# A meter for the projection work, and the written order on TensorE, in a hybrid HGRN2 + RWKV-7 layer

## The chip, the cores and the metric

The kernel runs on one core of a Trainium2 chip. A core has a matrix engine (TensorE, "PE" in the profile, with its weight loads as "PEld"), a vector engine (VectorE, "DVE"), an activation engine (ScalarE, "ACT"), GpSimd ("POOL") and a sync engine ("SP"). The last two are used here almost only to issue DMA transfers; a "q" behind an engine's name means its queue of transfers. The metric is the time of one execution in device microseconds, as the median of several runs; lower is better.

## What is computed

One decoder layer over 2048 tokens of width 1024, in float32. The input projection feeds two recurrent mixers side by side, HGRN2 (four heads of 128) and RWKV-7 (eight heads of 64). Their outputs go through an output projection; then comes a gated feed-forward network with a causal convolution of width 3.

```python
h = rmsnorm(x);  proj = h @ w_in            # 1024 -> 3840 columns
o_hg = hgrn2(q, f, i, g)                    # S_t = diag(f_t) S_{t-1} + k_t v_t^T ; o_t = S_t^T q_t
o_rw = rwkv7(r, k, v, wd, ad, gd)           # S_t = S_{t-1} diag(w_t) + (S_{t-1} a_t) b_t^T + v_t k_t^T
x = x + concat(o_hg, o_rw) @ w_out
x = x + conv_ffn(rmsnorm(x))                # 1024 -> 2 x 2816, conv over 3 tokens, SiLU gate, -> 1024
out = rmsnorm(x)
```

## The kernel before, in words

Tokens are worked on in four blocks of 512. To keep float32 precision with the fast matmul form, each operand of a projection is split into a high part (a copy on ScalarE) and a low part (a subtraction on VectorE); one product is then three matmuls of 128x512 (`mm3`, lines 259 to 261: high x high, high x low, low x high). Splits of weights are lines 243 and 244, other splits 236 and 237.

**Stage 1** (`phase1`) holds the input projections, both recurrences and the output projections of the first three blocks. Three generators are run against each other. Each `yield` ends a step.

- `dense()` goes through a list of jobs: 30 column blocks of the input projection for each token block ("P", eight steps of one `mm3` each, into the PSUM tag `pj`); transposes of the next block's input ("T", `turn`, line 428); the output projection of a finished block ("O", `out_block`, 32 steps of one `mm3` each); norms and transposes for stage 2 ("N"). Weights come by POOL's queue through tiles `wraw`/`woraw` and split tiles `wh` and `wl`, four buffers of each. `load(i)` fetches the two pairs of split tiles for column block `i`, one block ahead: read and split in the first token block, read back already split from DRAM in the later ones.
- `rw_super()` does RWKV-7 for one token block and four of the eight heads: eight such super steps, numbered 0 to 7 here, each a chain over all engines. Its main stations are: decay and keys (L647 to L694); scores `M` (matmuls L706, mask on VectorE L709); transposes (L731, L740, L745) and L757; the inverse of the triangular score matrices (below); L802, L815, L828 that put the inverse together and apply it; L852 with the VectorE evictions L855 and L858; L868 and L875 into two more PSUM banks; eight chunk steps (L886, with L888 on VectorE); then L896, L904, L916 and the output `yo` (L917, L918, stored by L919).
- `hg_unit()` does HGRN2 for one token block and one head: sixteen units, with VectorE products (L945 to L954), score matmuls (L970), transposes (L1012) and a state update (L1025).

**The inverse** is solved on VectorE with another layout than the scores have. Parts of `M` are stored to DRAM (`Ed`, L722) and read back as `E` (L725). A loop of 31 dependent pairs of VectorE instructions (L776, L778) makes `Ti`, with a `yield` after every fourth. `Ti` is stored (`T0d`, L782), and so is a transposed copy `TiT` (`T1d`, L785). Both are read back in the scores' layout, as `TZ` (L790, read by L802) and `TTs` (L794, read by L815 and L828). All these transfers are issued by SP in the order of the text.

**What sets the order.** The main loop takes one step of the RWKV-7 stream and one of the HGRN2 stream, then `fill(TICK)` takes steps of `dense()` worth 2000 ns of their own price (648 for an `mm3`, 680 in an output block, 436 for four transposes). A scheduler then orders each engine's instructions by its own estimate of when they are ready, TensorE's too, so that the order on an engine can differ from the text. An output block waits until both recurrences have finished its token block.

**Stage 2** begins with the output projection of the last block (`wacc`, its loads at L1153 from `oT`), then up-projection, convolution and down-projection, with a Strassen-like scheme. Its buffers lie where those of stage 1 lay.

Of the kernel before, what the change touches and what calls it, by code (L numbers as in the profile page):

```python
# [25 lines left out]
NFF = FF // P  # L26
TICK = 2000.0
NEG_C = -0.6065306597126334
# [30 lines left out]


@with_exitstack
def tile_layer(ctx, tc, consts, x, norm1_w, w_in, hg_lb_logits, hg_norm_w, rw_shift_mu, rw_w0, rw_w2,
# [3 lines left out]
    nc = tc.nc  # L66
    V, S, TE = nc.vector, nc.scalar, nc.tensor
    dma = nc.sync.dma_start
# [40 lines left out]
    def act(out_, in_, func, **kw):  # L109

        want = tables.get(func)
        if want is not None and want != tab["now"]:
            pre = S.preload_act_table_set(want)
            for u_ in tab["uses"]:
                tc.add_manual_dep(pre.ins, u_.ins.name, NOSYNC, reason="table order")
            tab.update(now=want, pre=pre, uses=[])
        i_ = S.activation(out_, in_, func, **kw)  # L117
        if want is not None:
            tc.add_manual_dep(i_.ins, tab["pre"].ins.name, NOSYNC, reason="table order")
            tab["uses"].append(i_)  # L120
        return i_
# [141 lines left out]
    def phase1(c1):  # L263
# [102 lines left out]

        def out_block(nb, oh=None, ol=None, then=None):


            for i2 in range(2):  # L370
                for dh in range(2):
                    accs = [bank("pj") for _ in range(2)]
                    for k in range(KD):
# [16 lines left out]
                        for q in range(2):  # L390
# [4 lines left out]
                            if i2 == 1 and dh == 1 and q == 1:  # L395
                                next_block(then, k)
                            yield 680
                    for q in range(2):
# [100 lines left out]
        def dense():  # L499
# [64 lines left out]
            for n, jb in enumerate(jobs):  # L564
# [14 lines left out]
                if jb[0] in "OW":  # L579
                    while done["rw2"] < 2 * jb[1] + 2 or done["hg"] < 4 * jb[1] + 4:  # L580
                        yield None
                    if jb[0] == "W":
                        jb[2]()
                    else:
                        yield from (out_block(2, *rows["O"]) if jb[1] == 2 else out_block(jb[1], then=jb[1] + 2))
                    continue
# [5 lines left out]
                if i == 0:  # L592
                    next(ahead)
                    next(ahead)
                    constants()
                load(i + 1)
                i += 1
# [32 lines left out]
        def rw_super(nb, s_):  # L630
# [84 lines left out]
            Ed = dp.tile([64, 32, 32], F32, tag="Ed", name="Ed", bufs=2)  # L715
            T0d = dp.tile([2, 64, 32, 16], F32, tag="T0d", name="T0d", bufs=2)
            T1d = dp.tile([64, 16, 2, 32], F32, tag="T1d", name="T1d", bufs=2)
# [6 lines left out]
            for f in range(2):  # L724
                dma(E[64 * f:64 * f + 64], Ed)  # L725

            KBT = tile_("KBT", [2, 8, P], "KBT")
# [53 lines left out]
            TiT = rp.tile([P, 16, 32], F32, tag="E", name="TiT")  # L781
            dma(T0d.rearrange("f m t c -> (f m) t c"), Ti)  # L782
            act(TiT, Ti.rearrange("m a b -> m b a"), AF.Copy)
# [3 lines left out]
            for e in range(2):  # L787
                r0 = er0(e)
                for f in range(2):
                    dma(TZ[r0:r0 + 32, 0].rearrange("p u b h t -> p (u b h) t")[:, :, 16 * f:16 * f + 16],  # L790
                        T0d[f, 32 * e:32 * e + 16].rearrange("m t c -> t m c"))
                for q in range(2):
                    m0 = (e * 2 + q) * 16
                    dma(TTs[r0 + 32 * q:r0 + 32 * q + 32, :, 32 * q:32 * q + 32],  # L794
                        T1d[m0:m0 + 16].rearrange("m c f t -> (c f) m t"))
            for _ in range(2):
                yield
            z = bank2()
# [278 lines left out]

        while any(alive.values()):
            for key, g in (("r", rw_), ("h", hg_)):
                if alive[key]:  # L1080
                    try:
                        next(g)
                    except StopIteration:
                        alive[key] = False
            fill(TICK)


    if "1" in stages:
        with ExitStack() as c1:
            phase1(c1)  # L1090
# [420 lines left out]
```

## Time and profile before

| | |
|---|---|
| median of 3 runs | 2753.06 us (2752.97 to 2757.32) |
| the profiled execution | 2757.5 us, of which the span from first to last instruction is 2755.7 us |
| TensorE busy | 96% of the span |
| VectorE busy | 69% |
| ScalarE busy | 49% |
| mean granted TensorE clock | 0.983 |

A page of the profile names engines as above and source lines as L12. "Idle before" is time in which an engine did nothing before an instruction, put down to what ended it. Ends of matmuls are modelled, and matmuls overlap in the pipeline, so the start of the next one tells more of a matmul's cost than its own duration. The chain of waits is followed back from the last instruction, at each step to whatever released it. Views by stretch give each engine's busy microseconds, then the clock that TensorE was granted (1.00 is full), then the share of DMA time and GB/s.

### The profile page before, as it was taken

The page shows a single profiled execution, that of the slowest core. Times are in us where ns is not written, and L with a number is a line of the kernel's source. Part 1 is how long each engine was busy: PE and PEld are TensorE (multiplying, and loading weights), DVE is VectorE, ACT ScalarE, POOL GpSimd, SP SyncE. Part 2 cuts the span into 40 slices and gives each one's busy share as a digit, 9 for nine tenths or more (in the row PEclk, how much of TensorE's full clock was granted, in tenths as well). Part 3 has the DMA queues.
Part 4 walks back from the last instruction along what each step waited for, and adds up shares of the span by engine and source line. Part 5 has one row for each costly group of instructions (what it writes and reads, how often), then busy time and mean ns, then how long its engine had stood idle before and what let it go on. Part 6 is the DMA issues. An engine that isn't in the chain of part 4 may idle for free.

```text
span 2755.7 us, 47958 instructions
## 1 busy us (share of the span) xinstructions
PE 2647.8 (96%) x18059; PEld 2107.5 (76%) x18059; DVE 1898.6 (69%) x3665; ACT 1350.4 (49%) x2164; POOL 368.3 (13%) x660
## 2 busy tenths in 40 slices
PE   7999999989999999999989999998999999999998
PEld 6777777767777767778667788886888888877887
DVE  4856556565456664657657889988997786667656
ACT  5546443444544444344446755455455555445444
POOL 6433222212321113222100000000000000000000
PEclk9999999999999999999999999999999999999999
DMA  8645544355663546844575367746662224999865
GB/s 301 202 152 166 165 138 131 115 146 173 217 176 104 152 146 203 286 138 123 161 273 160 114 205 258 242 148 218 223 228 77 88 85 144 327 327 313 285 196 184
DMA packets 364285, 515.78 MB, mean 187 GB/s; under 512 B 97311, under 2 KB 193941, under 8 KB 364053
## 3 DMA queue, kind: packets, MB, share of 16 engines
q1 hardware_dynamic: 312113, 343.29, 38.6%
q0 software_dynamic: 51872, 169.41, 18.9%
q8 instruction: 142, 2.33, 0.3%
q14 instruction: 90, 0.74, 0.1%
q10 hardware_dynamic: 68, 0.02, 0.0%
HBM read 375.22 MB, written 137.36 MB: 186 GB/s over the span
## 4 chain that ended last, share of the span: by engine, by line
PE 73%; DMA 8%; DVE 7%; issue 5%; ACT 4%; SPq 1%; POOL 1%; DVEq 0%; ACTq 0%; POOLq 0%
PE pj L259 8%; PE pj L260 7%; PE pj L261 7%; PE ua L261 5%; PE ua L259 5%; PE ua L260 5%; PE ud L259 3%; PE ud L260 3%; PE ud L261 3%; PE da L260 2%; PE da L261 2%; PE da L259 2%; PE hg L970 2%; PE db L259 2%; PE db L261 2%
## 5 line engine op out<-in xcount | busy, mean ns | idle before, releaser
L259 PE MATMUL pj<-hh,wh 128*128 128x512 f32 x960 | 404.9, 422 | 0.7 <-ACT hh L117 0.7
L261 PE MATMUL pj<-hh,wl 128*128 128x512 f32 x960 | 380.6, 397 | 0.0
L260 PE MATMUL pj<-hl,wh 128*128 128x512 f32 x960 | 380.6, 397 | 0.0
L259 PE MATMUL ua<-Bh,uwh 128*128 128x512 f32 x704 | 278.6, 396 | 13.8 <-ACT uwh L243 13.1
L261 PE MATMUL ua<-Bh,uwl 128*128 128x512 f32 x704 | 276.9, 394 | 0.9 <-DVE uwl L244 0.9
L260 PE MATMUL ua<-Bl,uwh 128*128 128x512 f32 x704 | 276.4, 393 | 0.0
L259 PEld LDWEIGHTS pj<-hh,wh 128*128 128x128 f32 x960 | 182.4, 190 | 54.2 <-issue 11.8
L260 PEld LDWEIGHTS pj<-hl,wh 128*128 128x128 f32 x960 | 182.6, 190 | 39.7 <-issue 6.2
L261 PEld LDWEIGHTS pj<-hh,wl 128*128 128x128 f32 x960 | 182.2, 190 | 40.1 <-issue 0.4
L243 ACT CAST uwh<-uraw 128x512 fp32r<-128x512 f32 x220 | 134.8, 618 | 145.9 <-PE ua L260 73.2
L243 ACT CAST dah<-draw 128x512 fp32r<-128x512 f32 x151 | 93.8, 621 | 184.1 <-PE da L260 50.5
L244 DVE TENSOR_TENSOR uwl<-uraw,uwh 128x512 fp32r<-128x512 f32 x220 | 146.7, 684 | 47.5 <-ACT uwh L243 47.3
L244 DVE TENSOR_TENSOR dal<-draw,dah 128x512 fp32r<-128x512 f32 x151 | 104.0, 689 | 107.3 <-ACT dah L243 107.2
L259 PEld LDWEIGHTS ua<-Bh,uwh 128*128 128x128 f32 x704 | 133.6, 190 | 43.1 <-ACT uwh L243 13.7
L261 PEld LDWEIGHTS ua<-Bh,uwl 128*128 128x128 f32 x704 | 133.5, 190 | 30.6 <-DVE uwl L244 2.7
L260 PEld LDWEIGHTS ua<-Bl,uwh 128*128 128x128 f32 x704 | 133.6, 190 | 27.3
L259 PE MATMUL ud<-Bh,uwh 128*128 128x512 f32 x352 | 137.9, 392 | 1.9 <-DVE cv L1362 1.9
L261 PE MATMUL ud<-Bh,uwl 128*128 128x512 f32 x352 | 137.1, 389 | 0.0
L260 PE MATMUL ud<-Bl,uwh 128*128 128x512 f32 x352 | 137.0, 389 | 0.0
L260 PE MATMUL da<-dbl,dah 128*128 128x512 f32 x340 | 133.8, 394 | 0.6 <-DVE dbl L244 0.5
L261 PE MATMUL da<-dbh,dal 128*128 128x512 f32 x340 | 133.3, 392 | 0.0
L259 PE MATMUL da<-dbh,dah 128*128 128x512 f32 x340 | 128.3, 391 | 2.4 <-ACT dbh L243 2.3
(558 smaller groups left out, 6036.7 us busy)
## 6 DMA issues: line engine op xcount, KB each, us to landing
uraw<-in_w_up_dram SPq DMA_DIRECT2D x176, 256.0 KB, 3.3
woraw<-in_w_out_dram POOLq DMA_DIRECT2D x96, 256.0 KB, 3.6
draw<-Sg SPq DMA_DIRECT2D x88, 256.0 KB, 3.1
draw<-Tw SPq DMA_DIRECT2D x88, 256.0 KB, 3.0
gd<-y SPq DMA_DIRECT2D x86, 256.0 KB, 2.9
xt<-x1d SPq DMA_DIRECT2D x32, 512.0 KB, 6.0
draw<-gd SPq DMA_DIRECT2D x63, 256.0 KB, 4.8
draw<-in_w_down_dram SPq DMA_DIRECT2D x63, 256.0 KB, 5.3
```

The costliest lines, as they stand in the source:

```text
L243: S.copy(hi, src)
L244: V.tensor_sub(lo, src, hi.bitcast(F32))
L259: TE.matmul(acc, lh, rh, start=first, stop=False, skip_group_check=skip)
L260: TE.matmul(acc, lh, rl, start=False, stop=False, skip_group_check=skip)
L261: TE.matmul(acc, ll, rh, start=False, stop=last, skip_group_check=skip)
L970: TE.matmul(o, kt[:, t0:t0 + 64], qs, start=True, stop=True, tile_position=(0, e * 64))
```

## The change

Four things are changed; the arithmetic is the same.

1. The order of TensorE's instructions in stage 1 is the order in which the text issues them. The other engines are ordered by the scheduler as before.
2. The projection work of a tick is no longer a constant 2000 ns. A wrapper around VectorE adds up an estimate for each instruction issued (150 ns plus 1.04 ns an element of a row), half that for each ScalarE activation, and 8000 ns at two places where `rw_super` sends data through DRAM. A tick then grants 900 ns plus 0.45 of what the two recurrence steps of this tick have added. One of two empty steps ahead of L802 is gone.
3. `T0d` has the two halves of a row next to each other. The store of `Ti` becomes two transfers with pieces of 64 bytes, the four loads of `TZ` become two with pieces of 128 bytes, and all of them are issued ahead of the four loads of `TTs`.
4. The weights of the column block that follows an output block are no longer loaded ahead of that block, but in its last quarter, three steps of eight before the end.

```diff
-TICK = 2000.0
+FLOOR, RATE = 900.0, 0.45
+OP_NS, ELEM_NS, TRIP_NS = 150.0, 1.04, 8000.0
...
+def width(ap):
+    n = 1
+    for d in ap.shape[1:]:
+        n *= d
+    return n
+
+class Metered:
+    def __init__(self, engine):
+        self.engine, self.ns = engine, 0.0
+
+    def __getattr__(self, name):
+        call = getattr(self.engine, name)
+
+        def f(out_, *args, **kw):
+            self.ns += OP_NS + ELEM_NS * width(out_)
+            return call(out_, *args, **kw)
+
+        return f
...
-    V, S, TE = nc.vector, nc.scalar, nc.tensor
+    S, TE = nc.scalar, nc.tensor
+    V = Metered(nc.vector)
...
+        V.ns += 0.5 * (OP_NS + ELEM_NS * width(out_))
         i_ = S.activation(out_, in_, func, **kw)
...
-        def out_block(nb, oh=None, ol=None, then=None):
+        def out_block(nb, oh=None, ol=None, then=None, last=None):
...
                             if i2 == 1 and dh == 1 and q == 1:
                                 next_block(then, k)
+                                if k == KD - 3 and last is not None:
+                                    last()
...
-                        yield from (out_block(2, *rows["O"]) if jb[1] == 2 else out_block(jb[1], then=jb[1] + 2))
+                        yield from (out_block(2, *rows["O"]) if jb[1] == 2 else
+                                    out_block(jb[1], then=jb[1] + 2, last=lambda: load(i)))
...
-                load(i + 1)
+                kinds = [jb_[0] for jb_ in jobs[n + 1:]]
+                if "O" not in kinds[:kinds.index("P") if "P" in kinds else 0]:
+                    load(i + 1)
...
-            T0d = dp.tile([2, 64, 32, 16], F32, tag="T0d", name="T0d", bufs=2)
+            T0d = dp.tile([64, 32, 2, 16], F32, tag="T0d", name="T0d", bufs=2)
...
             for f in range(2):
                 dma(E[64 * f:64 * f + 64], Ed)
+            V.ns += TRIP_NS
...
-            dma(T0d.rearrange("f m t c -> (f m) t c"), Ti)
+            for f in range(2):
+                dma(T0d[:, :, f, :], Ti[64 * f:64 * f + 64])
             act(TiT, Ti.rearrange("m a b -> m b a"), AF.Copy)
...
-                for f in range(2):
-                    dma(TZ[r0:r0 + 32, 0].rearrange("p u b h t -> p (u b h) t")[:, :, 16 * f:16 * f + 16],
-                        T0d[f, 32 * e:32 * e + 16].rearrange("m t c -> t m c"))
+                dma(TZ[r0:r0 + 32, 0].rearrange("p u b h t -> p (u b h) t"),
+                    T0d[32 * e:32 * e + 16].rearrange("m t f c -> t m (f c)"))
+            for e in range(2):
+                r0 = er0(e)
                 for q in range(2):
                     m0 = (e * 2 + q) * 16
                     dma(TTs[r0 + 32 * q:r0 + 32 * q + 32, :, 32 * q:32 * q + 32],
                         T1d[m0:m0 + 16].rearrange("m c f t -> (c f) m t"))
-            for _ in range(2):
-                yield
+            V.ns += TRIP_NS
+            yield
...
         while any(alive.values()):
+            t0 = V.ns
...
-            fill(TICK)
+            fill(FLOOR + RATE * (V.ns - t0))
...
-        with ExitStack() as c1:
+        with ExitStack() as c1, tc.manual_schedule(engines={mybir.EngineType.PE}):
             phase1(c1)
```

## The prediction

> **What bounds the kernel now.** I read the page first, then the waits of TensorE, then the stretches with a low granted clock, then the instructions in order of time at three places.
>
> ```profile
> span 2755.7 us, 47958 instructions
> PE 2647.8 (96%) x18059; PEld 2107.5 (76%) x18059; DVE 1898.6 (69%) x3665; ACT 1350.4 (49%) x2164; POOL 368.3 (13%) x660
> ```
>
> TensorE is the bound, so a change that leaves its 18059 matmuls alone can only win what TensorE loses: idle time, half clock, and matmuls that run long. Stage 2's instructions are the same in both programs, so all of it must come from stage 1 and its end, about the first 1400 us. The idle time, by what ended it:
>
> ```profile
> PE pj L259 <- ACT wh L243: 14.7, 12, 4.3
> PE rw L802 <- DMA TZ<-T0d: 14.3, 9, 4.3
> PE rw L868 <- DVE AR L858: 8.9, 6, 2.2
> PE wacc L259 <- ACT Bh L236: 7.3, 1, 7.3
> PE hg L1012 <- DVE hk L1005: 3.9, 1, 3.9
> PE rw L815 <- ACT TZ L117: 2.0, 4, 0.5
> ```
>
> Columns: us in total, times, longest. Five places hold most of it: split output weights (L259), the solved inverse coming back from DRAM (L802, L815: 16.3 us), PSUM banks after L858, and the border to stage 2. The clock comes on top:
>
> ```profile
> 157.00:171.00 14.00, 14.00 (x182) 9.86 (x180) 6.43 (x18) 10.52 (x26) 2.33 (x4) 0.52 0.30 114
> 597.00:611.00 14.00, 9.72 (x179) 6.91 (x179) 5.48 (x15) 4.56 (x12) 0.95 (x2) 0.53 0.60 126
> 1384.00:1405.00 21.00, 13.74 (x47) 10.39 (x46) 12.07 (x18) 8.90 (x14) 1.27 (x2) 0.76 0.66 231
> ```
>
> Columns: stretch, length, busy us of PE, PEld, DVE, ACT, POOL, then granted clock. Around the L802 steps of two super steps the clock is half; 14 x (1 - 0.52) = 6.7 us is the most such a stretch costs.
>
> **Part 1: the written order on TensorE.** The scheduler of before moves projections in between the small matmuls. In the built programs the number of runs of 512-column projections that begin behind other work falls from 298 to 240 in stage 1. What a new run costs:
>
> ```profile
> 1371.49 0.72 PE rw L896 x18
> 1372.21 0.43 PE pj L259
> 1372.64 0.23 PE pj L260
> 1372.87 0.24 PE pj L261
> ...
> L259 PE MATMUL pj<-hh,wh 128*128 128x512 f32 x960 | 404.9, 422 | 0.7 <-ACT hh L117 0.7
> L260 PE MATMUL pj<-hl,wh 128*128 128x512 f32 x960 | 380.6, 397 | 0.0
> ```
>
> The chain of waits shows the first projection behind a small matmul at 0.43 us, its followers at 0.23: 0.20 us a run, 58 x 0.20 = 12 us saved. The lower bound is the group rows: L259, which begins each run, is busy 24.3 us more than L260, 0.08 a run over 298 runs, 5 us. I take 12, the single case seen directly. [...]
>
> L868 follows L852 with no projection between in six of eight super steps of before, and waits 8.9 us for the banks that L858 empties. The written order puts three projection steps or more there, of three matmuls each (9 x 0.23 = 2.1 us, against 1.5 us a wait). Gain 9; lower bound 4, if VectorE is behind.
>
> In exchange TensorE may no longer pass a matmul that isn't ready. Recurrence and HGRN2 matmuls of the same tick now hold up whatever is written behind them. Before shows this at one place only (L1012, 3.9 us once); between nothing and 4 us in each of the eight super steps, I take 5 in total, near the one row, and keep 0 to 32.
>
> **Part 2: the meter, and the inverse's round trip.** Each tick now grants 900 ns plus 0.45 of the VectorE time that the step is estimated to have issued, instead of 2000 ns. What counts is whether the work written between the score matmuls (L706) and L802 covers the chain behind L802: copy to DRAM and back, 31 dependent pairs on VectorE (L776, L778), and copy again. Super step 3:
>
> ```profile
> 546.46 1.29 DVE L709 TENSOR_TENSOR M<-rw,cst 128x512 f32<-128x512 f32 x2 [2.75 <-PE rw L706]
> 559.27 0.19 DVE L776 TENSOR_TENSOR etmp<-E,Ti 128x31 f32<-128x31 f32 x1
> 593.30 0.16 DVE L778 TENSOR_TENSOR Ti<-Ti,etmp 128x16 f32<-128x16 f32 x1
> ...
> 600.35 0.31 PE L802 MATMUL rw<-TZ,M 32*32 32x32 f32 x4 [0.34 <-DMA TZ<-T0d]
> 603.32 1.06 PE L802 MATMUL rw<-TZ,M 32*32 32x32 f32 x60 [2.65 <-DMA TZ<-T0d]
> ```
>
> ```profile
> 559.27:593.46 34.19, 33.33 (x255) 26.41 (x256) 30.84 (x110) 15.45 (x28) 7.09 (x13) 1.00 0.47 147
> ```
>
> So 11.5 us from the last mask product to the loop, 34.2 us of loop (VectorE busy for 30.84 of it, the third number behind the stretch's length), and 10 us from its end to the last L802 operand: 55.6 us in all, and 3.0 us of wait. The loop is long because other VectorE work stands in it:
>
> ```profile
> L244 DVE TENSOR_TENSOR wl<-woraw,wh 128x512 fp32r<-128x512 f32 x94 | 64.5, 688 | 46.9 <-ACT wh L243 46.2 <-ACT hv L117 0.2
> L778 DVE TENSOR_TENSOR Ti<-Ti,etmp 128x126 f32<-128x126 f32 (+22 forms) x248 | 62.4, 252 | 3.5
> L776 DVE TENSOR_TENSOR etmp<-E,Ti 128x126 f32<-128x126 f32 (+22 forms) x248 | 61.8, 249 | 15.5 <-DMA E<-Ed 12.2
> L945 DVE TENSOR_TENSOR hX<-hq,hf 128x256 f32<-128x256 f32 x112 | 46.9, 419 | 3.3 <-PE hg L970 2.8
> ```
>
> From the built programs: between L706 and L802 stand 1244 projection matmuls before and 1320 after over the eight super steps (+76 x 0.23 = +17 us of cover), but 123 fewer HGRN2 matmuls (about 0.09 us each, -11) and 29 fewer runs (-6). Cover in total is unchanged. Inside the loops the foreign VectorE instructions go from 335 to 311, but unevenly. In super step 1 they fall from 50 to 29. In steps 3 and 5 the projection side's rise from 12 to 23 and from 11 to 24, because the output block now falls into the loop: 11 to 13 more at 0.69 us less some HGRN2 work at 0.42 is 6 us more loop in each. Step by step, the old wait plus the loop's change minus the cover's change gives (0 to 7) 3, 0, 5, 8, 0, 4, 6, 0: 26 us against 14 before at L802. I book +12; the ends are -16 (all gone) and +35 (each step waits as step 3 does).
>
> **Part 3: the changed layout of the round trip.** One store of the inverse (256 KB) becomes two with 64-byte pieces; four loads become two with 128-byte pieces, and both now stand on SP ahead of the four L794 loads, which wait for a second store.
>
> ```profile
> T0d<-Ti SPq DMA_DIRECT2D x8, 256.0 KB, 2.1
> TZ<-T0d SPq DMA_DIRECT2D x32, 32.0 KB, 2.8
> DMA to landing us min/median/max: 2.9/3.6/4.0
> ```
>
> The last row is of the neighbour T1d, whose stores have 128-byte pieces. The new store resembles those more than the old one: I take 4 to 5 us to land, 2 to 3 more than 2.1. In return the second half of TZ is no longer queued behind L794 (2.65 us in the row of 603.32). Booked at 0, ends -3 and +3 us in each super step that waits. The L794 loads come later by two issues; L815 needs them after L802's matmuls, its operands' evictions and a projection step, which cover that.
>
> **Part 4: weights around the output blocks.** Before loads the next projection's weights ahead of each output block, and they hold two of four buffers through it; that is where most of L259's 14.7 us fall. After, four are free, and the load is issued three k-steps before the end. The third block has all four already and waits some 2 us; so I take 14.7 to 8, gain 7. Ends: 12 gained, or 5 lost if the late load (four transfers on POOL's queue) isn't there when the next projection starts. Late next is the split itself.
>
> **Part 5: the border.**
>
> ```profile
> 1390.16 0.39 PE L261 MATMUL pj<-wh,hl 128*128 128x512 f32 x1
> 1397.80 0.79 PE L259 MATMUL wacc<-woh,Bh 128*128 128x512 f32 x1 [7.25 <-ACT Bh L236]
> ...
> 1387.90 1.22 DVE L918 TENSOR_TENSOR yo<-rw,yo 128x1024 f32<-128x1024 f32 x1
> 1396.91 0.69 DVE L237 TENSOR_TENSOR wol<-Bl,woh 128x512 fp32r<-128x512 f32 x1 [5.64 <-ACT woh L236]
> ...
> 1394.03 3.02 DMA Bh<-oT
> ```
>
> In before the last work is the third output block, and stage 2's loads wait for its last matmul (3.02 us of landing in the open). After, that block is done first and the loads wait only for the matmul 36 places before the end, so they lie under the last recurrence steps. What remains open is L918 and two splits, 2.6 us, plus two ScalarE passes in the last super step that projections covered: 5 us against 7.25. With half of the 21 x 0.24 = 5 us of lost clock: gain 4.5 (0 to 10).
>
> **The sum**, against the profiled execution's 2757.5 us: -12 - 9 + 5 + 12 - 7 - 4.5 = -15.5, so 2742. The median shown lies 4.4 us below that execution, so 2737.
>
> **The rivals.** *The round trip is covered everywhere.* If the meter spreads the cover well and the loops with fewer foreign instructions (step 1) are typical, L802's 16 us go as well and nothing new waits: -12 - 9 - 12 - 4.5 - 16 = -54, 2700. Against it: steps 3 and 5.
>
> *VectorE becomes the bound of the recurrence (slower).* TensorE in order stands at an HGRN2 or output matmul whose operand is queued on VectorE in the loop; projections behind it, and so their evictions, come late, and with them the rest of the loop. It decides once the waits at and before L802 pass 16 + 33 + 6 = 55 us, 7 us a super step instead of 2. At 9 a step it is 72 - 16 - 33 = +23: 2776. For it: VectorE is busy for 30.84 of the 34.19 us loop shown; against it: the foreign instructions fall in sum.
>
> *The clock takes it back (no change).* Four waits of 4 us and more at L802 (steps 2, 3, 5, 6) could each bring a stretch as at 157 us: 4 x 6.7 less the two that before has already is +13, so 2751. [...]
>
> **How the numbers follow.** This kernel can tell about 0.2% (5.5 us) from no change. Forecast 0.42 (2737, own range 2722 to 2747), all covered 0.18, VectorE 0.28, clock 0.12. Faster 0.60, same 0.12, slower 0.28. The range of 2703 to 2775 leaves out the better part of "all covered" and the worse half of "VectorE".
>
> **What would show it.** Right: L868 and L259 nearly gone from the waits, fewer and longer runs of pj, wacc's first wait under 5 us, L802 at about 25 us with steps 3 and 5 longest. Wrong: waits of pj or hg on VectorE above 20 us in sum, L802 above 50, or new slices of low clock.

## The result, and the profile after

The changed kernel takes 2806.16 us (median of 4 runs, 2804.15 to 2808.43) against 2755.19 us for the kernel before on the same chip (median of 4, 2752.97 to 2760.16). The ratio is 1.0181, with a 95% interval of 1.0167 to 1.0196: slower, where 2737 was forecast. Its profiled execution has a span of 2805.7 us, 50.0 us more than before.

From the page of the changed kernel (busy time of each engine, share of the span, instructions):

```profile
PE 2643.6 (94%) x18059; PEld 2109.4 (75%) x18059; DVE 1910.3 (68%) x3665; ACT 1366.7 (49%) x2178; POOL 367.1 (13%) x660
```

TensorE is busy for 4.2 us less than before, and the span is 50.0 us longer: by this row all of the loss is waiting. (Busy time at half the clock counts as busy, though: in a row of the last section PE is busy for 3.40 of 3.40 us at a granted clock of 0.50.) Where the loss lies is seen from stage 1 alone, from 20 us to the first wacc matmul. One row of the windows view for each kernel gives the length, then the busy us of PE, PEld, DVE, ACT and POOL, then the granted clock. Before:

```profile
20.00:1397.80 1377.80, 1315.11 (x12240) 1017.54 (x12241) 834.35 (x2046) 624.89 (x1000) 353.65 (x633) 0.98 0.53 168
```

The changed kernel, the whole stage and then a stretch of 13.7 us in the first super step:

```profile
20.00:1445.00 1425.00, 1314.93 (x12252) 1023.26 (x12250) 844.57 (x2043) 643.08 (x1016) 352.57 (x632) 0.95 0.53 163
148.30:162.00 13.70, 3.26 (x73) 2.65 (x72) 2.27 (x7) 2.57 (x6) 3.00 (x5) 0.63 0.84 206
```

Stage 1 ends 47.2 us later; 2.8 us of the 50.0 are lost behind it. Its length splits into three parts, which I use for every kernel below: *idle* (length less busy TensorE: 62.7 before, 110.1 after), *half clock* (half of TensorE's busy time in the stretches that the records show at half the clock: 26.2 and 48.7) and the *remainder* (1288.9 and 1266.2). So by this split the changed kernel loses 47 us more to waits and 22 us more to the clock, and 23 us less are left for the matmuls at full clock: 47.4 + 22.5 - 22.7 = +47.2. Half is an upper bound, and every us too much in it is missing in the remainder; for the projections it is nearly reached, since in such a stretch one starts 0.43 us behind the other (median), and 0.23 us outside. The half clock comes in 20 stretches with 130 us in sum, against 11 with 63 us.

The waits of TensorE in the changed kernel (us in total, times, longest; L836 is before's L802, L285 to L287 are L259 to L261, L456 is L428, L886 is L852; all VectorE work carries the meter's L80):

```profile
PE rw L836 <- DMA TZ<-T0d: 40.7, 12, 10.1
PE pj L285 <- ACT wh L269: 16.2, 8, 5.3
...
PE pj L456 <- ACT xt L143: 8.2, 5, 3.8
PE pj L285 <- DVE hgg L80: 7.4, 3, 3.3
PE pj L286 <- DVE wl L80: 7.0, 15, 2.4
PE rw L886 <- ACT UV L143: 5.7, 2, 3.1
PE hg L279 <- DVE xt L80: 5.2, 3, 3.0
PE pj L285 <- DVE xh L80: 4.0, 2, 2.1
PE wacc L285 <- ACT Bh L262: 3.0, 1, 3.0
PE hg L1046 <- DVE hk L80: 2.9, 1, 2.9
PE pj L285 <- DVE Sc L80: 2.6, 1, 2.6
```

Set against the rows of before: the round trip at L802 rises from 14.3 to 40.7. The wait at L868 (8.9) is gone, since its successor L902 has no row any more. The split weights of projections and output blocks rise from 16.5 (14.7 on wh, 1.8 on wl) to 23.2. New are projection matmuls that wait until VectorE has emptied a PSUM bank (hgg, xh and Sc, 14.0 in sum; the Sc copy stands right behind an addition of xh, which empties the bank), the transposes of the next input, which wait for ScalarE's copies (L456: 8.2, before's L428 2.2), and matmuls of the recurrence whose operand is late (L886).

Two of these waits in order of time. First the longest one at L836. The chain in the queue of SP (start, length, issued work), where the inverse is done at 143.1 us:

```profile
143.15 4.63 SPq L815 DMA_DIRECT2D T0d<-Ti  x2
147.82 7.05 SPq L818 DMA_DIRECT2D T1d<-TiT  x2
156.75 0.84 SPq L822 DMA_DIRECT2D TZ<-T0d  x2
158.13 1.95 SPq L828 DMA_DIRECT2D TTs<-T1d  x4
```

and TensorE beside it:

```profile
148.32 0.39 PE L287 MATMUL pj<-hh,wl 128*128 128x512 f32 x1
158.76 0.32 PE L836 MATMUL rw<-TZ,M 32*32 32x32 f32 x4 [10.06 <-DMA TZ<-T0d]
```

The projections written between the score matmuls and L836 are used up at 148.7 us; the next instruction in the written order is L836, and TensorE stands for 10.06 us. The issue of the two stores takes 4.63 and 7.05 us of SP's time, and the loads stand behind them.

Second, the longest wait on split weights, in super step 7, where an output block lies in front of L836:

```profile
1371.97 0.54 POOL L409 DMA_DIRECT2D woraw<-in_w_out_dram  x1 [3.71 <-DVE wl L80]
1375.24 0.62 ACT L269 CAST wh<-woraw 128x512 fp32r<-128x512 f32 x1 [2.75 <-DMA woraw<-in_w_out_dram]
1375.89 0.69 DVE L80 TENSOR_TENSOR wl<-woraw,wh 128x512 fp32r<-128x512 f32 x1 [0.55 <-ACT wh L269]
...
1376.80 1.90 SPq L828 DMA_DIRECT2D TTs<-T1d  x4
1376.88 0.54 POOL L409 DMA_DIRECT2D woraw<-in_w_out_dram  x1 [4.37 <-DVE wl L80]
...
1378.74 0.96 SPq L429 DMA_DIRECT2D x1d<-xh  x2
1379.80 5.58 SPq L406 DMA_DIRECT2D oraw<-oT  x4
1383.03 0.40 ACT L262 CAST hh<-oraw 128x256 fp32r<-128x256 f32 x1 [7.17 <-DMA oraw<-oT]
1383.31 0.54 POOL L409 DMA_DIRECT2D woraw<-in_w_out_dram  x1 [5.89 <-DMA x1d<-xh]
1383.34 0.61 ACT L269 CAST wh<-woraw 128x512 fp32r<-128x512 f32 x1
```

One turn of a weight buffer runs POOL's issue, landing, ScalarE's copy, VectorE's subtraction, and then the next issue, which waits for that subtraction: from 1371.97 to 1376.88 it is 4.91 us. The four buffers of the ring serve the loads of the other half (oraw) and the output rows (xh) too. At 1376.80 SP is busy with the round trip's loads, xh is stored at 1378.74 and oraw is asked for at 1379.80, behind them. ScalarE waits 7.17 us for oraw, and the copy of the weights follows behind that split, at 1383.34. TensorE's matching row is "5.3" in the waits above. So the work that the meter gives as cover for the round trip is fed in part through the same SP queue as the round trip. No run moves these transfers to another queue, so what the sharing costs is not shown.

### The profile page after: what moved, and what is told of

The parts are those of the page before. It is cut to its first block, busy times and chain, and to the rows that moved or that the text cites. A ratio compares the mean times of both kernels' runs of the same rounds, so it can differ in the third digit from the quotient of the medians.

```text
span 2805.7 us, 47910 instructions
## 1 busy us (share of the span) xinstructions
PE 2643.6 (94%) x18059; PEld 2109.4 (75%) x18059; DVE 1910.3 (68%) x3665; ACT 1366.7 (49%) x2178; POOL 367.1 (13%) x660
## 4 chain that ended last, share of the span: by engine, by line
PE 41%; DMA 3%; DVE 3%; issue 1%; ACT 1%; SPq 1%; DVEq 0%; ACTq 0%
PE ua L285 5%; PE ua L287 5%; PE ua L286 5%; PE ud L285 3%; PE ud L286 3%; PE ud L287 3%; PE da L286 2%; PE da L287 2%; PE da L285 2%; PE db L285 2%; PE db L286 2%; PE db L287 2%; PE ub L285 1%; PE ub L287 1%; PE ub L286 1%
## 5 line engine op out<-in xcount | busy, mean ns | idle before, releaser
L285 PE MATMUL pj<-hh,wh 128*128 128x512 f32 x960 | 411.0, 428 | 0.1
L287 PE MATMUL pj<-hh,wl 128*128 128x512 f32 x960 | 380.2, 396 | 0.0
L285 PE MATMUL ua<-Bh,uwh 128*128 128x512 f32 x704 | 278.5, 396 | 16.2 <-ACT uwh L269 14.1
L287 PE MATMUL ua<-Bh,uwl 128*128 128x512 f32 x704 | 276.5, 393 | 0.5 <-DVE uwl L80 0.4
L285 PEld LDWEIGHTS pj<-hh,wh 128*128 128x128 f32 x960 | 183.6, 191 | 51.5 <-issue 8.8
L287 PEld LDWEIGHTS pj<-hh,wl 128*128 128x128 f32 x960 | 183.2, 191 | 40.9
L80 DVE TENSOR_TENSOR uwl<-uraw,uwh 128x512 fp32r<-128x512 f32 x220 | 146.7, 684 | 50.2 <-ACT uwh L269 50.1
L80 DVE TENSOR_TENSOR dal<-draw,dah 128x512 fp32r<-128x512 f32 x151 | 104.0, 689 | 103.9 <-ACT dah L269 103.5
L285 PEld LDWEIGHTS ua<-Bh,uwh 128*128 128x128 f32 x704 | 133.2, 189 | 45.7 <-ACT uwh L269 14.7
L287 PEld LDWEIGHTS ua<-Bh,uwl 128*128 128x128 f32 x704 | 133.2, 189 | 30.8 <-DVE uwl L80 2.8
L285 PE MATMUL ud<-Bh,uwh 128*128 128x512 f32 x352 | 137.9, 392 | 1.4 <-DVE cv L80 1.4
L287 PE MATMUL ud<-Bh,uwl 128*128 128x512 f32 x352 | 137.1, 389 | 0.0
L286 PE MATMUL ud<-Bl,uwh 128*128 128x512 f32 x352 | 137.0, 389 | 0.0
L80 DVE SCALAR_TENSOR_TENSOR y<-cv,cvt,y 128x1024 f32<-128x1024 f32 x88 | 112.5, 1278 | 33.9 <-ACT y L143 33.9
L287 PE MATMUL da<-dbh,dal 128*128 128x512 f32 x340 | 132.4, 390 | 0.0
```

What stands on the lines that cost most here:

```text
L80: return call(out_, *args, **kw)
L285: TE.matmul(acc, lh, rh, start=first, stop=False, skip_group_check=skip)
L286: TE.matmul(acc, lh, rl, start=False, stop=False, skip_group_check=skip)
L287: TE.matmul(acc, ll, rh, start=False, stop=last, skip_group_check=skip)
```

## The experiments

All ratios are to the kernel before, measured beside it on the same chip, with their 95% interval. The letters in the expectations name theories: A, the written order itself costs; B, the meter puts the work in the wrong places; C, the store of the new layout costs; D, the layout is a trade and the loop is what is late; E, the output weights' VectorE work lengthens the inversion loop; F, the round trip lacks cover; G, the ring of raw weight buffers turns too slowly; H, the splits stand in the engines' queues behind the recurrences.

### The written order alone

```
-        with ExitStack() as c1:
+        with ExitStack() as c1, tc.manual_schedule(engines={mybir.EngineType.PE}):
```

The kernel before with this line alone.

> The kernel before with one line changed: TensorE keeps the written order in stage 1; constant ticks, old layout and old weight load stay. Theory A (TensorE in written order cannot fill the wait for the inverse's round trip at L802, and the meter only softens that): 1073 dense matmuls' time is written where the scheduler had put 40 us more, so the idle time ahead of L802 grows from 24 us (last score matmul to L802, eight super steps) to 60 or more, and the time is 2790 to 2830. Rival B (the meter itself puts the work in the wrong places, the written order is harmless): 2745 to 2765.

Measured: 2825.98 us, ratio 1.0253 [1.0230, 1.0275]. Its first wait:

```profile
PE rw L802 <- DMA TZ<-T0d: 87.3, 16, 12.7
```

Before, the scheduler put projections into the round trip wherever L802 wasn't ready; in the written order with 2000 ns a tick, the round trip is open for 87.3 us instead of 14.3. Stage 1 has 137.0 us of idle time (62.7 before); TensorE's busy time falls by 12.0 us and the remainder by 15.3. Theory A's figures are met, B's are not: the written order alone costs more than the whole change, and under it the rest of the change wins 0.72% back, some 20 us.

### Everything but the written order

```
-        with ExitStack() as c1, tc.manual_schedule(engines={mybir.EngineType.PE}):
+        with ExitStack() as c1:
```

The changed kernel with this line alone.

> The changed kernel without the written order: the scheduler may move TensorE's instructions again; meter, layout and late load stay. Theory A: the scheduler fills most of the wait, 2750 to 2780, above before only by the longer round trip of the new layout. Rival B (the meter's distribution costs the time): 2790 or more. The saving by fewer runs of projections goes away too (about 286 runs instead of 240).

Measured: 2776.69 us, ratio 1.0068 [1.0045, 1.0091]. With the scheduler back, the same meter leaves these waits:

```profile
PE rw L836 <- DMA TZ<-T0d: 20.2, 5, 6.8
PE pj L285 <- ACT wh L269: 15.0, 18, 2.3
```

The time is within A's figures. Taking the written order out wins 1.13%, some 31 of the 50 us. Idle time is 82.8 us and the remainder is nearly that of before (1287.9), so the 15 to 23 us by which the remainder falls belong to the written order. What stays of the change still costs 0.7% under the scheduler: the eight inversion loops take 287 us together, against 255 before, and 28.5 us are lost on operands and PSUM banks of projections and output blocks, against 17.9.

### The old layout of the round trip, in the changed kernel

```
-            T0d = dp.tile([64, 32, 2, 16], F32, tag="T0d", name="T0d", bufs=2)
+            T0d = dp.tile([2, 64, 32, 16], F32, tag="T0d", name="T0d", bufs=2)
...
-            for f in range(2):
-                dma(T0d[:, :, f, :], Ti[64 * f:64 * f + 64])
+            dma(T0d.rearrange("f m t c -> (f m) t c"), Ti)
```

with the four old TZ loads and their place.

> The changed kernel with the old layout of T0d and the old order of its loads; everything else stays. Theory C (the new store with its 64-byte pieces costs SP 2.4 to 4.7 us of issuing instead of 0.3 and delays L802's first operands from 8.9 to 12.9 us behind the loop in the mean): TensorE in order then waits 3 to 4 us less in each super step, 2775 to 2785. Rival D (the loop on VectorE is what is late; the layout is a trade, since the second half of TZ comes earlier): within 5 us of 2806.

Measured: 2804.34 us, ratio 1.0169 [1.0151, 1.0186], within the interval of the changed kernel. The wait at L836 is 39.2 us instead of 40.7. The old layout lets the first L836 group start earlier and its last group no sooner: from the end of the loop to the last L836 group it takes 95.1 us over super steps 0 to 6 with the new layout and 95.0 us with the old one. Rival D's figure is met.

### The old place of the weight load, in the changed kernel

```
-                kinds = [jb_[0] for jb_ in jobs[n + 1:]]
-                if "O" not in kinds[:kinds.index("P") if "P" in kinds else 0]:
-                    load(i + 1)
+                load(i + 1)
```

and no `last` at the output blocks.

> The changed kernel with the weights of the column block behind an output block loaded ahead of that block again. If the four free buffers help as the prediction said, this costs 5 to 10 us: 2811 to 2816. If the late load was itself late (TensorE waits for split weights were 16.2 us, no fewer than before), it gains: 2796 to 2803. If the output blocks are held by VectorE's and POOL's queues instead, no change within 3 us.

Measured: 2814.2 us, ratio 1.0206 [1.0187, 1.0224]; idle time 116.4 us against 110.1. The late load is worth 0.25%, some 7 us, though the ends of the two intervals overlap. In the traces it shows more clearly: without it TensorE waits 44.9 us for wh and wl, with it 23.2.

### The output weights without their subtractions

```
-                        wh, wl = split(wp, raw, [P, 512], "w", 4)
+                        wh = wp.tile([P, 512], F32R, tag="wh", name="wh", bufs=4)
+                        S.copy(wh, raw)
+                        wl = wh
```

Once in the changed kernel, and once in the kernel before as a control.

> The changed kernel with the low half of the output weights left out: the high half is used twice, so TensorE's 18059 matmuls stay, and 96 VectorE subtractions of 0.69 us go (66 us of VectorE; a part of the computation is left out). Theory E (the meter puts output blocks into the stretch of the loop, and their splits on VectorE lengthen the loop they should cover): the loops of super steps 3, 5, 6 and 7, now 38 to 42 us, fall to 31 to 35, and the time to 2775 to 2785. Rival F (too little work is written ahead of L802, whatever stands in the loop): the loops shorten, but the time falls by no more than 8 us.

> The same edit on the kernel before, as the control (a part of the computation is left out here too). Theory E: only super steps 3 and 5 have some of these splits in their loop, so the gain is 0 to 8 us (2747 to 2755). If the gain is as large as in the changed kernel, these splits cost the same under either order and explain nothing of the difference.

Measured: 2780.6 us, 1.0103 [1.0074, 1.0131] for the changed kernel, and 2733.16 us, 0.9928 [0.9906, 0.9951] for the control. The 96 subtractions cost 21 us under the written order (0.78%) and 20 us in the kernel before (0.72%), so they do not make the difference between the two. In the changed kernel the loops of super steps 3, 5 and 7 do get shorter, from 42.4, 41.3 and 41.8 us to 23.6, 33.4 and 28.5 us; that of step 6 does not (38.4 to 39.7). Yet idle time falls only from 110.1 to 106.2 us:

```profile
20.00:1419.70 1399.70, 1293.48 (x12245) 1010.40 (x12245) 788.34 (x1945) 641.38 (x1014) 351.61 (x629) 0.97 0.53 165
```

Busy time falls by 21.5 us with the same matmuls, and the half-clock part by 19.3 (48.7 to 29.4): most of the gain is clock. In the control it is similar: busy time falls by 22.5 us, and the half-clock part by 13.9 of them. Theory E's figure for the time is met, and it is right about three of the four loops, but the control shows that this is not the loss. (The three matmuls of a product also read one weight tile here instead of two; the runs do not set this apart from the subtractions.)

### More cover for the round trip

```
-            V.ns += TRIP_NS
+            V.ns += 3 * TRIP_NS
```

in the changed kernel, at the second place (behind the TTs loads): by 0.45 of 16 us, some 7 us more work in each round trip.

> The changed kernel with three times the constant at the second round trip (24000 instead of 8000 ns), which writes about 8 us more projections ahead of L802 in each super step. Rival F: the idle time ahead of L802, 78 us in the changed kernel, falls by 45 to 60 us and the time to 2750 to 2770. Theory E: more work ahead of L802 is again output blocks in three of the super steps; the waits move to split weights and the time falls by no more than 25 us, or rises as the last super steps lack cover.

Measured: 2780.96 us, ratio 1.0105 [1.0073, 1.0136].

```profile
PE pj L285 <- ACT wh L269: 20.8, 17, 6.7
...
PE pj L285 <- DVE xh L80: 11.8, 9, 2.5
...
PE pj L286 <- DVE wl L80: 8.9, 22, 1.5
...
PE rw L836 <- DMA TZ<-T0d: 5.9, 1, 5.9
```

The wait at L836 is nearly gone (40.7 to 5.9), which shows that the cover was too short. But only 14.5 of these 34.8 us leave the idle time (110.1 to 95.6). In their place the output blocks and projections wait for weights (23.2 to 29.7) and for PSUM banks (xh: 4.0 to 11.8). Another 16 us leave the half-clock part (48.7 to 32.3). By the ratios the time falls by 21 us. That and the waits moved to split weights are what E said. F is right about the missing cover and misses both of its figures: the time is not 2750 to 2770, and all idle time from the last score matmul to L836 falls from 78 to 57 us, not by 45 to 60.

### The late load in the kernel before, and the TZ loads first

The kernel before with the hunks on `last` and `kinds` of the change alone; then the same, with the TZ loads moved ahead of the TTs loads in the old layout:

```
                         T0d[f, 32 * e:32 * e + 16].rearrange("m t c -> t m c"))
+            for e in range(2):
+                r0 = er0(e)
                 for q in range(2):
```

> The kernel before with the late load of the weights behind an output block alone. In the changed kernel this part was worth 6 us. If it is worth the same here: 2746 to 2751, with the waits for split weights (14.7 us) down to 8 or less. If the scheduler had already covered most of it: within 3 us of before.

> The kernel before with the late load and with the four loads of TZ issued ahead of those of TTs (old layout). The second half of L802's operands should come 3 to 5 us sooner after the loop; the scheduler covers most of that, so beside the late load alone (0.9972) I expect 0.994 to 0.997, with the wait of L802 for TZ (11.4 us with the late load alone) at 5 to 9 us. If the scheduler had covered all of it: 0.996 to 0.998.

Measured: 2744.35 us, 0.9972 [0.9955, 0.9989] for the late load, and 2741.59 us, 0.9951 [0.9936, 0.9966] with the order of the loads. The late load wins 8 us under the scheduler as well and so beats both kernels; its wait for wh falls only from 14.7 to 11.6, where 8 or less was expected. The order of the loads can't be told from it: the intervals overlap, and the wait at L802 is 12.4 us, against 11.4 with the late load alone and 5 to 9 expected (the trace is of the longest of its runs, 2751.63 us).

### Five raw weight buffers instead of four

```
-                        raw = wp.tile([P, 512], F32, tag="wraw", name="woraw", bufs=4)
+                        raw = wp.tile([P, 512], F32, tag="wraw", name="woraw", bufs=5)
```

and so for all tiles of this tag: in the changed kernel, in the kernel with more cover, and in the kernel before with the late load.

> The changed kernel with five buffers instead of four for the raw weights and rows (tag wraw). Theory G (TensorE in order stands in the output blocks because the ring of raw weights turns too slowly: issue on POOL, landing, copy on ScalarE, subtraction on VectorE): TensorE's waits for split operands in stage 1, 39 us, fall to 25 to 32, and the time by 8 to 15 us, 2790 to 2798. Rival H (the copies and subtractions stand in ScalarE's and VectorE's queues behind work of the recurrences): waits and time stay within 4 us.

> Both: the larger constant at the second round trip, which left 53 us of waits for split operands and 6 at L802, and five buffers. Theory G: 2755 to 2770, for the ring was what the larger cover ran into. Rival H: 2776 to 2785, as without the fifth buffer.

> The kernel before with the late load and five buffers. There the waits for split operands are 14 us in stage 1 with the late load. Theory G: 2 to 6 us less than the late load alone, ratio 0.995 to 0.997; rival H: 0.997 as the late load alone.

Measured: 2795.9 us, 1.0152 [1.0128, 1.0175]; 2763.19 us, 1.0029 [1.0014, 1.0045]; 2734.77 us, 0.9931 [0.9912, 0.9950]. With more cover and the fifth buffer:

```profile
PE rw L836 <- DMA TZ<-T0d: 13.1, 3, 7.6
...
PE pj L285 <- ACT wh L269: 8.7, 7, 2.8
```

By the ratios the fifth buffer alone wins 8 us (the wait on wh falls from 16.2 to 9.3, that at L836 rises to 48.2), more cover alone 21 us, and both together 42 of the 50 us lost. G's figure for the pair is met. For the fifth buffer alone G's time is met just so (8 to 15 us), its waits are not: those of the pj matmuls fall to 33, not to 25 to 32. The written order with both repairs is still 0.3% above the kernel before. In the kernel before with the late load the fifth buffer takes the weights out of the waits:

```profile
PE rw L807 <- DMA TZ<-T0d: 16.1, 9, 3.9
...
PE rw L873 <- DVE AR L863: 13.6, 8, 2.6
...
PE pj L259 <- ACT wh L243: 2.1, 4, 0.8
```

It is the fastest of the kernels that leave nothing out, 0.69% under the kernel before. By the ratios it wins 11 us beside the late load alone, more than G's 2 to 6. In the two traces stage 1 ends 6.4 us sooner, and little of that is idle time (60.7 to 58.2): other waits take most of the place of those for weights, and the half-clock part falls by 4.7. TensorE's first two waits in stage 1 are now the round trip and the banks of L868 (here L873), which the written order had removed.

The three parts of stage 1 for nine of these kernels (us; "trip" is the wait at L802 or L836, "pj" the waits of projections and output blocks for operands or PSUM banks, without the transposes; both lie inside idle):

| kernel | end of stage 1 | idle | trip | pj | half clock | remainder |
|---|---|---|---|---|---|---|
| before | 1397.8 | 62.7 | 14.3 | 17.9 | 26.2 | 1288.9 |
| changed | 1445.0 | 110.1 | 40.7 | 39.4 | 48.7 | 1266.2 |
| written order alone | 1460.1 | 137.0 | 87.3 | 21.9 | 29.5 | 1273.6 |
| no written order | 1410.7 | 82.8 | 20.2 | 28.5 | 20.0 | 1287.9 |
| more cover | 1417.7 | 95.6 | 5.9 | 53.3 | 32.3 | 1269.8 |
| five buffers | 1438.1 | 111.5 | 48.2 | 33.4 | 45.5 | 1261.1 |
| more cover, five buffers | 1403.2 | 86.2 | 13.1 | 36.2 | 35.2 | 1261.9 |
| before, late load | 1385.1 | 60.7 | 11.4 | 13.8 | 22.0 | 1282.4 |
| before, late load, five buffers | 1378.7 | 58.2 | 16.1 | 7.6 | 17.3 | 1283.2 |

## Why the prediction was wrong

The bound was named rightly: TensorE, and within it what stage 1 loses. The sum of -15.5 became +50 on the profiled executions. By its own terms, from the waits of the two kernels and the parts of stage 1:

| term | booked | measured | from |
|---|---|---|---|
| fewer runs of projections | -12 | -7 | projections at full clock, 859.7 to 852.9 |
| all other matmuls | 0 | -16 | the rest of the remainder, 1288.9 to 1266.2 |
| L868 | -9 | -9 | 8.9 us, now without a row |
| others waiting in order | +5 | +27 | all waits not named elsewhere, 12.7 to 39.7; of these PSUM banks of pj 0.6 to 14.0 |
| round trip (L802, L815) | +12 | +24 | 16.3 to 40.7 |
| weights around output blocks | -7 | +7 | wh and wl, 16.5 to 23.2 |
| border (waits) | -2 | -2 | 7.3, now 3.0 and two waits of 1.1 and 1.3 |
| clock | -2.5 | +22 | half-clock part, 26.2 to 48.7 |

The measured terms add up to +46, where stage 1 has +47.2 (small waits are left out, before and after). Four terms failed: the clock by 25 us, the waits in order by 22, the weights by 14 and the round trip by 12. Behind the round trip and the waits in order stands one step: the waits and the cover of the scheduled kernel were taken as what the written order would find. The weights and the clock failed by steps of their own.

*Part 1, written order.* The term is of the right sign, and its price was too high. I took 0.43 us for the first projection of a run from one place. Over stage 1, outside the half clock, the first one starts its follower after 0.34 us in both kernels (median), and the others after 0.23: 0.11 us a run, 6 us for the 57 fewer runs that the traces show (297 to 240). The projections together take 7 us less. That the remainder falls by 23 us in sum is luck: 16 us of it lie in the other, mostly small matmuls, and no run shows why. L868 went as said. The step that failed here is "between nothing and 4 us in each of the eight super steps, I take 5 in total": I went by the one wait that before shows at such a place (L1012). But before has so few because its scheduler fills them, so that row did not show what the written order would find. The end of 32 that I kept was nearly reached.

*Part 2, meter and round trip.* The step that failed is "Cover in total is unchanged". It counted the projections from the last score matmul to the first L802, and the traces give the same 1244 and 1320. But the chain ends with the last L802 group. Before, the scheduler put another 118 projections between the first and the last group; in the written order there is none. Up to the last group it is 1362 before and 1320 after, and the HGRN2 matmuls there fall from 1328 to 1062. No row shows the 0.09 us that the prediction took for an HGRN2 matmul: there, the next matmul starts after 0.053 us in the mean of before, and 0.052 in the changed kernel. At 0.053 that is 42 x 0.23 + 266 x 0.053 = 24 us less cover, where it booked none. The loops take 281 us in sum, against 255, 26 us more. Together that is 50 us; idle time between the last score matmul and the last L802 group goes from 24 to 78 us, 54 more. The experiments show the same from the other side. The written order alone leaves 1029 projections there, 333 x 0.23 = 77 us less than before, and waits 73 us more at L802; and 7 us more work in each round trip take 35 us of the changed kernel's 41 away.

Steps 3 and 5 were named as the longest loops, rightly (42.4 and 41.3 us, from 34.2 and 31.8), but step 7 grows as well (34.7 to 41.8), and I had left it at 0. The waits at L802 were expected where the loop is longest, and came elsewhere. By super step, 0 to 7, they are 10.4, 3.2, 7.3, 0.7, 5.5, 3.9, 9.7 and 0.0 us, where 3, 0, 5, 8, 0, 4, 6 and 0 were expected. In steps 3, 5 and 7, where output blocks are the cover, TensorE idles 14.8, 10.8 and 12.6 us on the way from the scores to the last L802 group, but only 4.6 us of this 38 at L802. Most of it goes to the output blocks' own weights and to PSUM banks.

*Part 3, layout.* Booked at 0 with ends of 3 us a step; the experiment gives 3 us in sum, inside its error. The part on the store was too low, though: I took 4 to 5 us to land and nothing for SP. The one new store whose landing the trace tells took 6.7 us, and the two issues hold SP for 2.3 to 4.6 us.

*Part 4, weights.* The late load is worth 7 to 8 us in both orders, as said. But the term had a second half that I did not price: the output blocks' own weights, once the meter runs these blocks fast inside the round trip. That step failed: 20.6 of the 23.2 us of these waits lie in the round trips of super steps 3, 5 and 7. "Late next is the split itself" was the right name, without a number.

*Part 5, border.* The 7.25 us wait became 3.0 us, but wol (1.7) and two yo passes of the last super step (L938, L950: 1.1 and 1.3) are now open, together 7.1. The two ScalarE passes cost what the working left for them (5 - 2.6 = 2.4). L918 and the two splits were priced too low, 2.6 us against 4.7. The wait on wol lies behind the end of stage 1.

*Clock.* The prediction took 2.5 us of gain and kept the loss as a rival of +13. Measured is +22. The step that failed is that only waits of 4 us and more were given a price in clock. No run shows a border there: in before, the stretches that begin at 157.4 and 597.8 us have no idle gap of TensorE above 2.52 and 1.29 us in the 16 us ahead. In the changed kernel, the stretch from 151.8 to 165.5 us begins inside the wait of 10.06. But others follow waits of under 2.1 us only (those from 332.7, 633.1, 657.0, 971.0 and 988.1 us, looking back 16 us). What the traces show instead is in the last section: half clock followed all 147 windows of 3.41 us in which TensorE was busy for less than 0.4; the idle time was in one piece around 151.8 us (10.06 us) and in two around 332.7 (1.70 and 1.54). In the prediction's row of 157 us TensorE is busy for all 14.00 us at a clock of 0.52; the window just ahead of that stretch is busy for 1.41 of 3.41 us. So in these traces the clock term goes with the waits. In the kernel without subtractions it falls by 19 us at nearly the same idle time, with 12 stretches in place of 20.

*The rivals.* "VectorE becomes the bound" had the side and the point of decision: 78 us of waits at and before L802, where 55 decide; by its own sum that gives some 2782, and measured is 2806. Its mechanism holds for the 14.0 us of PSUM banks. The larger part is another one: TensorE reaches L802 too early in the written order, and what covers it waits for its own weights. Of the signs of being wrong, the new stretches of low clock came, and the waits of pj and hg on VectorE above 20 us; L802 stayed under 50 at 40.7.

## What to carry to other kernels

A written order on an engine needs cover for each long round trip at the place where it is written. The waits of a scheduled kernel don't tell how much, because its scheduler has filled them: run the written order alone first, and read the wait there. Count the cover up to the last matmul that needs the round trip, not to the first. Work given as cover is worth only what its own supply allows, so look at which queue and buffers feed it and whether the round trip holds the same ones. Here a later load and one more raw buffer under the scheduler give 0.9931 [0.9912, 0.9950], and the written order with its two repairs only 1.0029. Short waits came with half clock here as a long one did (no wait above 1.94 us in the 16 us ahead of the stretch at 633.1 us, one of 10.06 us around 151.8 us), and with 47 us more idle time the changed kernel lost 22 us to the clock. So where a kernel waits in many places, read the granted clock beside the waits.

## What the hardware showed unexpectedly

The issue of the two stores with 64-byte pieces held SP for up to 4.02 us each here. The tile view of T0d in the changed kernel (ns at least, median, most):

```profile
L815 SPq DMA_DIRECT2D T0d<-Ti x16: 545/556/4024, 143.1 to 1369.6; - x16
```

and in the kernel before:

```profile
L782 SPq DMA_DIRECT2D T0d<-Ti x8: 320/326/343, 140.6 to 1315.6; - x8
```

Half of the data in 64-byte pieces takes 556 ns to issue (median) and up to 4024, where the whole in one store took 326; the pair of a super step takes 2.3 to 4.6 us, and what is issued behind it on SP starts later. That the size of the pieces is the cause is not shown: the stores of T1d, with the same pieces in both kernels, take up to 5157 ns in the changed kernel and up to 1462 before. The old layout in the changed kernel was no faster, so this did not decide the time.

In stage 1 the granted clock falls to half for stretches of 3.4, 6.8, 10.2 and 13.7 us, in steps of 3.41 us, and mostly without a wait of that length in front: 14 of the 20 stretches of the changed kernel have no idle gap of TensorE of 3.41 us or more in the 16 us ahead. One begins 3.1 us into the wait of 10.06 us; ahead of the one at 633.1 us, no wait above 1.94 us lies in these 16 us. Rows of the windows view (stretch, length, busy us of the five engines, granted clock), first the 3.41 us ahead of three stretches, then the stretch at 633.1 us itself:

```profile
148.41:151.82 3.41, 0.30 (x2) 0.00 (x0) 0.00 (x0) 1.21 (x2) 1.60 (x3) 1.00 1.02 304
629.69:633.10 3.41, 1.47 (x7) 0.77 (x6) 3.28 (x8) 1.54 (x3) 0.65 (x2) 1.00 0.57 148
967.62:971.03 3.41, 1.93 (x36) 1.63 (x33) 2.95 (x10) 2.33 (x5) 0.54 (x1) 1.00 0.55 168
633.10:636.50 3.40, 3.40 (x9) 2.72 (x9) 2.17 (x5) 1.15 (x3) 0.60 (x2) 0.50 0.86 296
```

and in the kernel before, ahead of the stretch at 157 us:

```profile
154.04:157.45 3.41, 1.41 (x63) 1.09 (x63) 0.69 (x1) 1.24 (x3) 1.08 (x2) 1.00 1.08 374
```

TensorE is busy for 0.30 to 1.93 of 3.41 us ahead of them, a share of at most 0.57. All fourteen traces of this case agree, from 20 to 1440 us. In each of them the stretches begin on one grid of 3413 ns, to 1.1 ns. Sorted by the share that TensorE is busy, this many of the grid's windows at full clock are followed by half clock:

| busy share of the window | windows | followed by half clock |
|---|---|---|
| under 0.4 | 147 | 147 |
| 0.4 to 0.5 | 38 | 26 |
| 0.5 to 0.6 | 75 | 12 |
| above 0.6 | 5191 | 4 |

Of the windows at half clock, all 129 that were busy for less than 0.8 were followed by another one at half, and 46 of the 232 busier ones. So in these traces half clock goes with the busy share of a window on this grid, not with the length of one wait. Between 0.4 and 0.6 both outcomes occur (38 of 113 followed by half clock) and no run shows what separates them; the four exceptions above 0.6 are open too.
